# A fourth place for raw U tiles during the selection, paid for with two smaller buffers

## The chip, the cores and the metric

The kernel runs on one core of a Trainium2 chip. What counts is the device time of one execution in microseconds (us); the median of three runs is compared. The engines are named as the profile names them: PE (TensorE matmul), PEld (its weight loads, which overlap), DVE (VectorE), ACT (ScalarE), POOL (GpSimd) and SP (SyncE, which issues most of the transfers).

## The reference, cut to what matters

Two trunk layers of a decoder run over 544 tokens (512 of a prompt, 32 of samples). Each layer is a mixer block followed by PEER, a layer of 16384 single-neuron experts of which every token picks 128. The change lies in PEER alone:

```python
q = (h @ w_q).reshape(B, T, PEER_HEADS, 2, PEER_HALF)
s = jnp.einsum('bthpc,hpkc->bthpk', q, subkeys)
s_top, i_top = lax.top_k(s, PEER_TOPK)            # 16 of 128 keys, for each half
...
best, pos = lax.top_k(cand, PEER_TOPK)            # 16 of the 256 pairs
idx = jnp.take_along_axis(cidx, pos, axis=-1)     # expert = key1 * 128 + key2
gate = jax.nn.softmax(best, axis=-1)
...
a = jnp.einsum('td,thed->the', xb, jnp.take(U, ib, axis=0))
wgt = gb * jax.nn.gelu(a)
return jnp.einsum('the,thed->td', wgt, jnp.take(V, ib, axis=0))
```

## The kernel before, in words

PEER treats its tokens in two ways. The first 384 tokens go through all experts densely: `gelu(U h)` is computed for each of the 128 tiles of U (tile k holds the 128 experts whose second key is k), multiplied by a matrix G of gates that is zero where an expert was not picked, and multiplied by V. The other 160 tokens fetch the rows of U and V that they picked, with indirect transfers from POOL (`gather`, five row buffers `g_r` of 128 x 1024 f32, 4 KB a partition each).

In each layer the order is as follows. `scores` computes the keys' scores and first top-16 lists. `second_stage` picks the 16 pairs of each head; it runs once for the gathered tokens and then three times, for 128 dense tokens each. After each of these three, `make_g` builds the columns of G: for 16 chunks of 8 tokens DVE makes four f16 tiles of 2 KB a partition: `ohp` (first key's one-hots), `ohq` (second key's), `ohh` and `ohl` (`ohq` times the high and the low part of the gate). PE multiplies `ohp` with `ohh` and `ohl` (L1467, L1468). `ohq` is read by DVE alone. The results pass through the tile `stage` to DRAM (`gd`), and through DRAM back into `gt`.

This stretch is called the selection here. To keep PE busy in it, `spend` strews two other kinds of work into the program: U tiles (`a_early`) and steps of the gather. A U tile is one transfer of 512 KB into a raw tile `wr` (L105, from SP), one cast `wh` on ACT (L98), one difference `wl` on DVE (L99), and 24 matmuls on PE (L118). `wr` has three places, `wh` and `wl` two each. The result passes through gelu (L1020) into the tile `kept` or, in groups of four, to DRAM (`ad`, L1027). The first 8 raw tiles of U are loaded beforehand into places of their own (`pre`). After the last `make_g` a loop runs `a_early` until 96 tiles are done (L1116 to L1117); the other 32 are done in the dense stage.

The dense stage takes the 128 tiles of V, one a step: a raw tile `vr` (L1183, three places), its split `vh`, `vl` (two places each), a gated tile of activations split into `gwh`, `gwl`, and 18 matmuls (L1199). Activations that went to DRAM come back as `gr` (L1168) with their gates `gt` (L1165). In the gather, `use` forms the dot products of the rows of U with h (L1268): the products are written to the tile `g_junk`, which nobody reads; the sum over the row goes to one column of `g_w`.

The kernel is written for a framework that places tiles in memory pool by pool, adds the waits, and writes each engine's instructions in an order that a planner fixes when the kernel is built; the planner may take an instruction ahead of earlier ones. On the chip every engine, and SP's queue of transfers, works strictly in that order. A tile that lies where an earlier, closed pool lay waits for the last use of what lay there.

The pools of the selection lie one on the other from `vi` (`val`, `idx`) over `sp` (the second stage's tiles) to `mg` (`make_g`'s tiles: four small ones, `stage` twice 16 KB, then the one-hots). When they are closed, the dense stage's pools take the place from the bottom of `vi` on: `fn` (two accumulators of 4 KB), `dv` (`vr` 3 x 4 KB, `vh` 2 x 4 KB, `vl` 2 x 4 KB), `dn` (`gwh`, `gwl`, `gt`, `gr`).

Of the kernel before, what the change touches and what calls it, by code (L numbers as in the profile page):

```python
# [9 lines left out]
F32 = mybir.dt.float32  # L10
F32R = mybir.dt.float32r
F16 = mybir.dt.float16
U32 = mybir.dt.uint32
AF = mybir.ActivationFunctionType
OP = mybir.AluOpType
AX = mybir.AxisListType

P = 128
L = 2
D = 1024  # L20
# [15 lines left out]
NKEY = 128  # L36
# [43 lines left out]
class Body:  # L80
# [917 lines left out]

    def a_fetch(self):
        k = self.a_next  # L1000
        self.a_w = self.weights(self.a["u"][self.a_l, k], wr=self.pre.pop(k, None)) if k < NKEY else None

    def a_tile(self, psum, ahead):

# [41 lines left out]
    def peer(self, l):  # L1046
        nc, a = self.nc, self.a
        gd = self.dp.tile([ND // ST, P, P, ST], F32, name=f"gd{l}")
        self.ad = self.dp.tile([P, NKEY // GA, GA, ND], F32, name=f"ad{l}")
        self.a_l, self.a_next, self.a_w = l, 0, None  # L1050
        self.pre = {}
        self.rows_due, self.rows_left = None, ROWPRE
        self.t_dve = self.t_pe = self.t_row = 0.0
        with ExitStack() as es:
# [7 lines left out]
            ve = ExitStack()  # L1062
# [3 lines left out]
            sp = self.pool("sp", ve)  # L1066
            ge = ExitStack()

            with ExitStack() as es2:
                hb = self.pool("hb", es2)  # L1070

                bh = hb.tile([P, NK, NQ], F32R, name="bh")
                bl = hb.tile([P, NK, NQ], F32R, name="bl")

                with ExitStack() as es3:
                    ns = self.pool("ns2", es3)
                    g = self.gains(ns, "g_ffn", l)

                    def sink(i, xt):
                        np_ = TILE[i]  # L1080
                        h = self.rownorm(ns, [xt], np_, g)
                        to = [(bh, bl, (i - 2) * P)] if i > 1 else []
                        to += [(self.ah, self.al, i * P)] if i < 3 else []

                        def put(k, pt):
                            for hi, lo, c in to:
                                self.split(hi[:, k:k + 4, c:c + np_], lo[:, k:k + 4, c:c + np_], pt)

                        self.to_feat(h, np_, 0, put)
                        if i == 3:  # L1090
                            nc.sync.dma_start(self.h2d[l][0], h)
                        elif i == 4:
                            for q in range(4):
                                nc.sync.dma_start(self.h2d[l][1, q * TS:(q + 1) * TS], h)

                    self.out_proj(l, ns, sink)
                self.hxs.close()
                sc = self.pool("sc", es2)
                pp = self.pool("pre", es2, side="right")
                self.pre = {k: pp.tile([P, D], F32, name=f"pre{k}") for k in range(PRE)}  # L1100
                self.scores(l, sc, val, idx, bh, bl)
                self.t_pe = 1e9
                self.second_stage(sp, val[:, 24:], idx[:, 24:], last)
                while self.pre:
                    self.a_early(len(self.pre) > 1)
            with ExitStack() as es2:
                mg = self.pool("mg", es2)
                gp = self.pool("gp", ge, side="right")
                self.rows_due = self.gather(l, gp, acc, last)
                self.t_dve = self.t_pe = self.t_row = 0.0  # L1110
                for i in range(ND // P):
                    F = [sp.tile([P, PH, TOPK], F32, name=f"sel{s}") for s in range(3)]
                    self.second_stage(sp, val[:, i * 8:i * 8 + 8], idx[:, i * 8:i * 8 + 8], F)
                    self.make_g(l, mg, gd, i, F)
            while self.a_next % GA or self.a_next < APRE:
                self.a_early(self.a_next % GA != GA - 1)  # L1116
            ve.close()  # L1117
            fn = self.pool("fn", es)
            acc += [fn.tile([P, D], F32, name=f"g_acc{i}") for i in range(2)]
# [117 lines left out]
    def gather(self, l, gp, acc, last):  # L1237

        nc, a = self.nc, self.a
        h2t = []  # L1240
        for t in range(2):
            h2t.append(gp.tile([P, D], F32, name=f"h2t{t}"))
            nc.sync.dma_start(h2t[t], self.h2d[l][t])
        u, v = [], []
        for t, (b0, b1) in enumerate(((0, PH), (PH, PH + 2))):
            ns = (b1 - b0) * TOPK
            src = [x[:, b0:b1].rearrange("p h k -> p (h k)") for x in last]
            ef = gp.tile([P, ns], F32, name=f"g_ef{t}")
            nc.vector.tensor_scalar(ef, src[0], float(NKEY), float(l * NKEY * NKEY), op0=OP.mult, op1=OP.add)
            e = gp.tile([P, ns], mybir.dt.int32, name=f"g_e{t}")  # L1250
            nc.vector.tensor_add(e, ef, src[1])
            w = gp.tile([P, ns], F32, name=f"g_w{t}")
            for s in range(ns):
                u.append((0, t, s, e, w, src[2]))
                v.append((1, t, s, e, w, src[2]))
        jobs = u + v
        rows = []
        late = None

        def use(job, r):  # L1260
            nonlocal late
            which, t, s, e, w, g = job
            if late is not None and s % TOPK == 2:
                nc.vector.tensor_mul(*late)
                late = None
            if which == 0:
                jk = gp.tile([P, D], F16, name="g_junk", bufs=1)
                ins = nc.vector.scalar_tensor_tensor(jk, r, 1.0, h2t[t], op0=OP.mult, op1=OP.mult,  # L1268
                                                     accum_out=w[:, s:s + 1])
                self.tc.keep_in_program_order(ins)  # L1270
                if s % TOPK == TOPK - 1:
                    ws = w[:, s + 1 - TOPK:s + 1]
                    nc.scalar.activation(ws, ws, AF.Gelu_apprx_tanh)
                    late = (ws, ws, g[:, s + 1 - TOPK:s + 1])
            else:
                nc.vector.scalar_tensor_tensor(acc[t], r, w[:, s:s + 1], acc[t], op0=OP.mult, op1=OP.add)  # L1276

        def run():
            for n in range(len(jobs) + GR - 1):
                if n < len(jobs):  # L1280
                    which, t, s, e, w, g = jobs[n]
                    r = gp.tile([P, D], F32, name="g_r", bufs=GR)
                    nc.gpsimd.indirect_dma_start(out=r, out_offset=None,  # L1283
                                                 in_=a["v" if which else "u_rows"].rearrange("l e d -> (l e) d"),
                                                 in_offset=bass.IndirectOffsetOnAxis(ap=e[:, s:s + 1], axis=0))
                    rows.append(r)
                if n >= GR - 1:
                    use(jobs[n - GR + 1], rows.pop(0))
                yield

        return run()
# [141 lines left out]
    def make_g(self, l, sp, gd, i, F):  # L1433
# [13 lines left out]
        for c in range(0, P, OHT):  # L1447
            if c % ST == 0:
                stage = sp.tile([P, P, ST], F32, name="stage", bufs=2)

            sh = [P, OHT // 2, P, 2]

            def row(t):
                return t[:, c:c + OHT].rearrange("p (b t) -> p b t", t=2)[:, :, None, :].to_broadcast(sh)

            keys = self.io[:, None, :, :].to_broadcast(sh)
            p_, q_, qh, ql = (sp.tile(sh, F16, name=n, bufs=2) for n in ("ohp", "ohq", "ohh", "ohl"))
            nc.vector.tensor_tensor(p_, keys, row(i1), op=OP.is_equal)
            nc.vector.tensor_tensor(q_, keys, row(i2), op=OP.is_equal)
            nc.vector.tensor_tensor(qh, q_, row(gh), op=OP.mult)  # L1460
            nc.vector.tensor_tensor(ql, q_, row(gl), op=OP.mult)
            self.spend(dve=2.9)
            for b in range(0, OHT, 4):
                ps = self.bank(2).rearrange("p (t j) -> p t j", t=4)
                for t in range(4):
                    w, half = (b + t) // 2, t % 2
                    nc.tensor.matmul(ps[:, t], p_[:, w, :, half], qh[:, w, :, half], start=True, stop=False)  # L1467
                    nc.tensor.matmul(ps[:, t], p_[:, w, :, half], ql[:, w, :, half], start=False, stop=True)  # L1468
                o = (c + b) % ST
                nc.scalar.activation(stage[:, :, o:o + 4].rearrange("p j t -> p t j"), ps,  # L1470
                                     AF.Copy, scale=1.0 / GSCALE)
            self.t_pe += 1.0
            if (c + OHT) % ST == 0:
                t = i * P + c + OHT - ST
                k = self.kept[:, :, t:t + ST]
                nc.vector.tensor_mul(k, k, stage[:, :KJ])
                nc.scalar.dma_start(gd[t // ST, :, KJ:], stage[:, KJ:])
# [128 lines left out]
```

## Time and profile before

| | before |
|---|---|
| median of 3 runs | 3926.21 us (3915.0 to 3933.97) |
| profiled execution: time / span | 3939.12 us / 3937.3 us |
| PE busy | 3796.4 us, 96% |
| PEld busy | 3423.2 us, 87% |
| DVE busy | 2885.8 us, 73% |
| ACT busy | 1579.2 us, 40% |
| POOL busy | 1084.3 us, 28% |
| DMA | 936.55 MB, mean 238 GB/s |
| mean granted TensorE clock | 0.987 |

A busy share is an average over stages that have different limits, so the stretch in which a change works has to be looked at by itself. The selection of the first layer lies at about 880 to 1320 us of the span, that of the second at about 2810 to 3250 us; the dense stages follow each.

### The profile page before, as it was taken

Reading aid. Unit: us, or ns where it says so; the run is one execution under the profiler, and the core shown is the slowest. Engines: PE = TensorE matmul, PEld = TensorE weight load, DVE = VectorE, ACT = ScalarE, POOL = GpSimd, SP = SyncE. Lnnn points to the kernel's source line nnn. Section 1 sums busy time; section 2 is a strip of 40 time slices with the busy share of each in tenths; the row PEclk is TensorE's granted clock in tenths of the full one; section 3 lists DMA queues with packets and bytes.
Section 4 is the critical chain, followed back from the end, with each engine's and each line's share of the span. In section 5 each row is a group of like instructions: output and inputs, shape, how many; then the busy total and the mean of one; then the engine's idle time right before and its main releaser. Section 6 shows DMA issues by size and latency. Waiting matters only on the chain.

```text
span 3937.3 us, 66183 instructions
## 1 busy us (share of the span) xinstructions
PE 3796.4 (96%) x25676; PEld 3423.2 (87%) x25676; DVE 2885.8 (73%) x5799; ACT 1579.2 (40%) x2373; POOL 1084.3 (28%) x880
## 2 busy tenths in 40 slices
PE   8999999999999899999999999999999989999998
PEld 7999997999989788888789998879989888888886
DVE  5554436799998787888955444467999878788888
ACT  4532324344555333333344323343456543333333
POOL 0110100005353444444501110000164334444343
PEclk9999999999999999999999999999999999999999
DMA  7243215327889999999933322262478999999997
GB/s 261 87 145 109 66 55 192 137 70 276 307 302 354 348 359 331 337 354 350 383 127 126 128 87 63 76 239 70 152 284 290 336 364 349 343 338 344 346 349 280
DMA packets 334028, 936.55 MB, mean 238 GB/s; under 512 B 28784, under 2 KB 126448, under 8 KB 330384
## 3 DMA queue, kind: packets, MB, share of 16 engines
q1 hardware_dynamic: 232912, 527.52, 38.5%
q0 software_dynamic: 92160, 335.59, 23.3%
q10 hardware_dynamic: 8640, 69.21, 4.5%
q8 instruction: 201, 3.29, 0.3%
q14 instruction: 115, 0.94, 0.1%
HBM read 835.50 MB, written 96.70 MB: 237 GB/s over the span
## 4 chain that ended last, share of the span: by engine, by line
PE 83%; DVE 6%; DMA 5%; issue 3%; ACT 2%; SPq 1%; POOL 1%; DVEq 0%; POOLq 0%; ACTq 0%
PE mm L118 36%; PE mm L1199 17%; PE sm L1199 8%; PE sm L118 7%; DMA g_r<-u_rows,g_e 3%; PE mm L344 2%; PE sm L586 2%; DVE wl L99 1%; SPq L1168 1%; PE sm L1467 1%; PE sm L1468 1%; PE sm L529 1%; PE sm L1340 1%; POOL g_r L1283 1%; PE sm L344 0%
## 5 line engine op out<-in xcount | busy, mean ns | idle before, releaser
L1283 POOL DMA_INDIRECT g_r<-u_rows,g_e x320 | 532.1, 1663 | 1322.9 <-DVE g_junk L1268 596.6
L98 ACT CAST wh<-wr 128x1024 fp32r<-128x1024 f32 (+1 forms) x464 | 466.2, 1005 | 945.5 <-PE mm L118 694.7
L99 DVE TENSOR_TENSOR wl<-wr,wh 128x1024 fp32r<-128x1024 f32 (+1 forms) x464 | 541.4, 1167 | 383.0 <-ACT wh L98 360.1
L118 PE MATMUL mm<-ah,wh 128*128 128x384 f32 (+1 forms) x1792 | 599.8, 335 | 29.3 <-ACT wh L98 22.8
L118 PE MATMUL mm<-ah,wl 128*128 128x384 f32 (+1 forms) x1792 | 603.1, 337 | 18.8 <-DVE wl L99 18.5
L118 PE MATMUL mm<-al,wh 128*128 128x384 f32 (+1 forms) x1792 | 594.3, 332 | 0.4 <-DVE al L99 0.4
L1283 POOL DMA_INDIRECT g_r<-v,g_e x320 | 440.6, 1377 | 525.8 <-DVE g_acc L1276 479.2
L1268 DVE SCALAR_TENSOR_TENSOR g_junk<-g_r,h2t 128x1024 f16<-128x1024 f32 x320 | 391.1, 1222 | 31.0 <-DMA g_r<-u_rows,g_e 29.7
L1276 DVE SCALAR_TENSOR_TENSOR g_acc<-g_r,g_w,g_acc 128x1024 f32<-128x1024 f32 x320 | 409.5, 1280 | 1.8 <-DMA g_r<-v,g_e 0.2
L118 PEld LDWEIGHTS mm<-ah,wh 128*128 128x128 f32 x1792 | 344.1, 192 | 37.1 <-ACT wh L98 24.9
L118 PEld LDWEIGHTS mm<-ah,wl 128*128 128x128 f32 x1792 | 343.0, 191 | 30.2 <-DVE wl L99 29.5
L118 PEld LDWEIGHTS mm<-al,wh 128*128 128x128 f32 x1792 | 343.7, 192 | 0.9 <-DVE al L99 0.9
L99 DVE TENSOR_TENSOR vl<-vr,vh 128x1024 fp32r<-128x1024 f32 x256 | 312.4, 1221 | 38.3 <-ACT vh L98 37.2
L118 PE MATMUL mm<-hh,wl 128*128 128x272 f32 x1536 | 332.4, 294 | 0.0
L118 PE MATMUL mm<-hl,wh 128*128 128x272 f32 x1536 | 330.9, 293 | 0.0
L118 PE MATMUL mm<-hh,wh 128*128 128x272 f32 x1536 | 328.5, 294 | 0.2 <-ACT hh L98 0.2
L1199 PE MATMUL mm<-vl,gwh 128*128 128x512 f32 x1024 | 317.4, 391 | 2.1 <-DVE vl L99 2.1
L1199 PE MATMUL mm<-vh,gwl 128*128 128x512 f32 x1024 | 316.3, 390 | 0.0
L1199 PE MATMUL mm<-vh,gwh 128*128 128x512 f32 x1024 | 281.0, 393 | 18.7 <-ACT vh L98 18.7
L98 ACT CAST vh<-vr 128x1024 fp32r<-128x1024 f32 x256 | 268.2, 1051 | 0.3 <-DMA vr<-v 0.3
L98 ACT CAST gwh<-gr 128x384 fp32r<-128x384 f32 x144 | 74.0, 514 | 447.9 <-PE sm L1199 447.9
L118 PEld LDWEIGHTS mm<-hl,wh 128*128 128x128 f32 x1536 | 242.8, 188 | 8.8 <-issue 6.7
(476 smaller groups left out, 7503.9 us busy)
## 6 DMA issues: line engine op xcount, KB each, us to landing
vr<-v SPq DMA_DIRECT2D x256, 512.0 KB, 6.8
wr<-u SPq DMA_DIRECT2D x240, 512.0 KB, 5.8
wr<-w_in SPq DMA_DIRECT2D x96, 512.0 KB, 3.5
gd<-stage ACTq DMA_DIRECT2D x24, 1664.0 KB, 8.9
gt<-gd SPq DMA_DIRECT2D x52, 768.0 KB, 7.8
ad<-ga ACTq DMA_DIRECT2D x36, 768.0 KB, 7.1
gr<-ad SPq DMA_DIRECT2D x36, 768.0 KB, 8.1
wr<-w_o SPq DMA_DIRECT2D x32, 512.0 KB, 3.5
```

The source lines that it names most:

```text
L98: self.nc.scalar.copy(hi, src)
L99: self.nc.vector.tensor_sub(lo, src, hi.bitcast(F32))
L118: nc.tensor.matmul(o, w[:, k * P:(k + 1) * P], x[part][:, k], start=(q == 0), stop=(q == 3 * nk - 1))
L344: nc.tensor.matmul(ps[i][s][:np_], m[:, k, c], w[:, s * 512:(s + 1) * 512], start=(k == 0 and q == 0), stop=(k == NK - 1 and q == 2))
L529: nc.tensor.matmul(ps[i], x[:, k, i * P:(i + 1) * P], w[:, kk * BW:(kk + 1) * BW], start=(k == 0 and q == 0), stop=(k == NK - 1 and q == 2))
L586: self.pairs_of(lambda b, lo, hi: nc.tensor.matmul(p[lo:hi, b], w[lo:hi, b], x(b, lo, hi), start=True, stop=True))
L1168: nc.sync.dma_start(ga4, self.ad[:, q])
L1199: ins = nc.tensor.matmul(po[i][s], w[:, i * P:(i + 1) * P], v[:, s * 512:(s + 1) * 512], start=(step == 1 and m == 0), stop=(step == NKEY ...
L1268: ins = nc.vector.scalar_tensor_tensor(jk, r, 1.0, h2t[t], op0=OP.mult, op1=OP.mult, accum_out=w[:, s:s + 1])
L1276: nc.vector.scalar_tensor_tensor(acc[t], r, w[:, s:s + 1], acc[t], op0=OP.mult, op1=OP.add)
L1283: nc.gpsimd.indirect_dma_start(out=r, out_offset=None, in_=a["v" if which else "u_rows"].rearrange("l e d -> (l e) d"), in_offset=bass.Ind ...
L1340: nc.tensor.matmul(ps[:, j, half], q[:, half, (i + j) * P:(i + j + 1) * P], sub[:, h * 2 + half], start=True, stop=True)
```

## The change

Three edits. A new pool `raw` with one tile of 128 x 1024 f32 (4 KB a partition) is opened between `sp` and `mg`. While it is open, every fourth tile of U (k = 11, 15, ... 95) is loaded into it instead of into one of the three places of `wr`. Its space comes from two others: `ohq` gets one buffer in place of two (2 KB), and `g_junk` (2 KB) goes away, the products of L1268 being written over the row `g_r` that they were formed from, in f32. `raw` is closed together with `vi` and `sp`, before the dense stage.

```diff
@@ a_fetch
         k = self.a_next
-        self.a_w = self.weights(self.a["u"][self.a_l, k], wr=self.pre.pop(k, None)) if k < NKEY else None
+        wr = self.pre.pop(k, None)
+        if wr is None and k < NKEY and k % 4 == 3 and self.raw is not None:
+            wr = self.raw.tile([P, D], F32, name="raw")
+            self.nc.sync.dma_start(wr, self.a["u"][self.a_l, k])
+        self.a_w = self.weights(self.a["u"][self.a_l, k], wr=wr) if k < NKEY else None
@@ peer
-        self.pre = {}
+        self.pre, self.raw = {}, None
...
                 while self.pre:
                     self.a_early(len(self.pre) > 1)
+
+            self.raw = self.pool("raw", ve)
             with ExitStack() as es2:
                 mg = self.pool("mg", es2)
...
             while self.a_next % GA or self.a_next < APRE:
                 self.a_early(self.a_next % GA != GA - 1)
+            self.raw = None
             ve.close()
@@ gather, use
-                jk = gp.tile([P, D], F16, name="g_junk", bufs=1)
-                ins = nc.vector.scalar_tensor_tensor(jk, r, 1.0, h2t[t], op0=OP.mult, op1=OP.mult,
+                ins = nc.vector.scalar_tensor_tensor(r, r, 1.0, h2t[t], op0=OP.mult, op1=OP.mult,
                                                      accum_out=w[:, s:s + 1])
@@ make_g
-            p_, q_, qh, ql = (sp.tile(sh, F16, name=n, bufs=2) for n in ("ohp", "ohq", "ohh", "ohl"))
+            p_, qh, ql = (sp.tile(sh, F16, name=n, bufs=2) for n in ("ohp", "ohh", "ohl"))
+            q_ = sp.tile(sh, F16, name="ohq")
```

## Rows read from the trace of the kernel before

**Rows 1.** The page's first line of engines: busy us (share) x instructions.
```profile
PE 3796.4 (96%) x25676; PEld 3423.2 (87%) x25676; DVE 2885.8 (73%) x5799; ACT 1579.2 (40%) x2373; POOL 1084.3 (28%) x880
```

**Rows 2.** Stretches of the first selection: length, busy by engine, clock, DMA share, GB/s.
```profile
960.00:980.00 20.00, 19.95 (x149) 18.70 (x148) 20.00 (x32) 14.11 (x18) 16.99 (x2) 1.00 0.63 227
...
1120.00:1140.00 20.00, 13.50 (x84) 12.72 (x84) 14.14 (x24) 6.30 (x9) 10.57 (x8) 0.83 0.89 327
...
1220.00:1240.00 20.00, 20.00 (x159) 19.37 (x158) 19.85 (x30) 13.15 (x17) 4.61 (x5) 1.00 0.91 335
```

**Rows 3.** Who waited for whom, 860 to 1325 us: total us, times, longest.
```profile
ACT wh L98 <- PE mm L118: 163.1, 72, 9.3
...
DVE g_junk L1268 <- DMA g_r<-u_rows,g_e: 16.0, 5, 5.9
...
ACT wh L98 <- DMA wr<-u: 12.7, 3, 8.4
...
PE sm L1467 <- DVE ohh L1460: 6.5, 1, 6.5
```

**Rows 4.** The passage to the dense stage, both layers: columns as in rows 2.
```profile
1265.00:1280.00 15.00, 12.89 (x61) 11.90 (x60) 7.10 (x8) 5.14 (x7) 4.72 (x3) 0.89 1.04 387
1280.00:1291.00 11.00, 2.08 (x8) 1.06 (x6) 3.37 (x6) 2.18 (x3) 0.00 (x0) 0.77 1.06 381
1291.00:1323.00 32.00, 30.49 (x157) 29.68 (x158) 24.23 (x36) 7.71 (x12) 14.80 (x12) 0.92 1.02 361
...
3212.00:3223.00 11.00, 2.74 (x9) 1.67 (x8) 3.69 (x6) 2.52 (x3) 0.00 (x0) 0.77 1.06 382
```

**Rows 5.** SP's queue in that passage, first layer: start, us, instruction, count.
```profile
1255.31 0.33 SPq L105 DMA_DIRECT2D wr<-u  x1
...
1257.53 15.95 SPq L1168 DMA_DIRECT2D gr<-ad  x1
...
1274.01 5.91 SPq L1168 DMA_DIRECT2D gr<-ad  x1
1280.02 0.97 SPq L105 DMA_DIRECT2D wr<-u  x2
1281.08 0.48 SPq L1183 DMA_DIRECT2D vr<-v  x1
```

**Rows 6.** ACT there: start, us, instruction, idle before and what ended it.
```profile
1288.52 1.04 ACT L98 CAST wh<-wr 128x1024 fp32r<-128x1024 f32 x1 [8.43 <-DMA wr<-u]
```

**Rows 7.** The chain that ended last: one U tile on PE.
```profile
1239.92 4.22 PE mm L118 x24
```

**Rows 8.** The dense stage's matmuls (L1199) alone in the passage: length, PE, PEld, clock, DMA.
```profile
1265.00:1280.00 15.00, 2.15 (x9) 1.79 (x10) 0.89 1.04 387
1280.00:1291.00 11.00, 0.95 (x5) 0.44 (x3) 0.77 1.06 381
```

**Rows 9.** DVE by line and shape: busy us, mean ns, idle before.
```profile
L99 DVE TENSOR_TENSOR wl<-wr,wh 128x1024 fp32r<-128x1024 f32 x416 | 508.6, 1223 | 371.7 <-ACT wh L98 348.9 <-ACT d_wt L662 16.8 <-PE sm L118 3.0
...
L1268 DVE SCALAR_TENSOR_TENSOR g_junk<-g_r,h2t 128x1024 f16<-128x1024 f32 x320 | 391.1, 1222 | 31.0 <-DMA g_r<-u_rows,g_e 29.7
...
L173 DVE SCALAR_TENSOR_TENSOR n_h<-x_o,rs_y,g_row 128x1024 f32<-128x1024 f32 x8 | 10.1, 1282 | 0.0
```

**Rows 10.** DVE in time: two chunks of make_g, first layer.
```profile
948.97 1.29 DVE L1459 TENSOR_TENSOR ohq<-io,i2T 128x1024 f16<-128x1024 f16 x2
...
955.02 1.29 DVE L1461 TENSOR_TENSOR ohl<-ohq,glT 128x1024 f16<-128x1024 f16 x2
```

**Rows 11.** DVE in time, after the second second_stage of the first layer.
```profile
994.25 1.23 DVE L1268 SCALAR_TENSOR_TENSOR g_junk<-g_r,h2t 128x1024 f16<-128x1024 f32 x1 [4.61 <-DMA g_r<-u_rows,g_e]
```

**Rows 12.** POOL in time, in two windows of the first selection.
```profile
964.85 25.61 POOL L1283 DMA_INDIRECT g_r<-u_rows,g_e  x1 [2.78 <-DVE gsum L1386]
...
1094.99 28.13 POOL L1283 DMA_INDIRECT g_r<-u_rows,g_e  x1 [3.93 <-DVE g_junk L1268]
```

**Rows 13.** A stretch of the first dense stage: columns as in rows 2.
```profile
1400.00:1500.00 100.00, 100.00 (x476) 86.52 (x475) 79.61 (x120) 33.40 (x47) 43.26 (x33) 1.00 0.97 350
```

## The prediction

> **What bounds the kernel now.** I read the page first: PE is busy for 96% of the span and no other engine for more than 87% [rows 1], so a change pays only where it fills a gap of PE. Next I cut the first selection into stretches of 20 us. PE and DVE are both full or nearly so in most of them, as at 960 and 1220 us, and 1120 to 1140 us is one of the few with a hole [rows 2]. The list of waits then says what raw tiles of U have to do with that: ACT's cast waits 72 times, 163.1 us, for PE to give back a place of `wh`, and only three times, 12.7 us, for the raw tile itself [rows 3]. So in the steady part the raw tile lies ready; three places are enough there. By SP's queue, the three late tiles all belong to the passage into the dense stage, after the last `make_g`. There PE is idle for 15.00 - 12.89 = 2.11, 11.00 - 2.08 = 8.92 and 32.00 - 30.49 = 1.51 us, 12.5 us in the first layer, and the granted clock falls (0.89, 0.77, 0.92: parts of the stretches run at 1.2 in place of 2.4 GHz); the second layer repeats it, with 8.26 us in the stretch in the middle [rows 4]. The queue shows why: one U tile leaves at 1255.31, then come the first loads of the dense stage, two `gr` among them that hold the queue for 15.95 and 5.91 us, and the next two U tiles leave at 1280.02 [rows 5]. DMA engines are full in this time (share 1.04 to 1.06 [rows 4]). ACT sits 8.43 us for that tile [rows 6], and PE behind it.
>
> **The fourth place.** A U tile costs PE 4.22 us [rows 7]. With four places the transfer of tile k waits for the split of tile k-4 in place of k-3, so each U tile stands one place further forward in SP's queue. Nothing is added to what is moved: the tile that leaves at 1255.31 is simply the next one by number. In the steady part this is worth nothing; what hides it is the wait of the cast for PE [rows 3]. At its first use, tile 11, the place waits for the scores' operand that lay there; the three tiles in `wr` before it cover that. Before the hold it gives PE one more tile to do: -4.2 us a layer.
>
> It also takes something away. In units of a partition's bytes, `vi` is 8704 and `sp` 14304, so `raw` lies from 23008 to 27104. The dense stage puts `fn` (8192) and three `vr` (12288) below, so its two `vh` lie from 20480 to 28672, and `raw` is under both. The last tile of the selection, 95, is a `raw` tile (95 = 3 mod 4). So the first two steps of the dense stage can't cast V before tile 95 has been split. Today some of their matmuls fill the hole: 2.15 + 0.95 = 3.1 us of PE in the two stretches [rows 8]. They will come later: +3.1 us. What is queued behind: `vl` on DVE and the next `vr`, which wait for these casts; the planner knows this wait and can put U's casts and loads ahead, so I add nothing for them. In turn those `vr`, as at 1281.08 [rows 5], no longer share the full DMA engines with U's tiles. Below, this is worth nothing; above, no more than the idle time that is left of the middle stretch, 8.9 - 4.2 + 3.1 = 7.8 us. Only two of the transfers then under way go, so I take a sixth, -1.3 us. Together: -4.2 + 3.1 - 1.3 = -2.4 us a layer, -4.8 us in both.
>
> What comes after keeps this gain: in the dense stage PE is busy for 98 to 100 of 100 us [rows 13], so work done earlier ends earlier.
>
> **One buffer for the second key's one-hots.** Writer and readers of `ohq` are all on DVE, which works in order, so no wait between engines is added. What changes is the order. Now `ohq` of two chunks is written in a row before either `ohl` [rows 10]; by DVE's rows 25 of the 48 chunks of a layer have it so. These must move behind the previous `ohl`. DVE's work is the same. Bounds a layer: if PE waited for every moved one, 25 times half of 1.29 us [rows 10], +16 us; if the new order took away PE's one long wait for `ohh`, -6.5 us [rows 3]. The rows stand near to zero: in 48 chunks PE has one long wait of this kind, and it comes when DVE itself stands for a gathered row. I take 0.
>
> **Products written over the rows.** 320 instructions write f32 where they wrote f16, in place. With f16 one takes 1222 ns; a difference of two f32 tiles written in f32-sized words takes 1223; a product with a column of scalars, written as f32, 1282 [rows 9]. So it is between 0 and 60 ns each, 0 to 19 us of DVE in all. L1268 has no column operand, so I take 0. The row buffer is given back by the same instruction as before, so the gather's transfers don't wait longer.
>
> **Sum.** 3939.1 us for the profiled execution, less 4.8, is 3934.3. That execution lies 12.9 us above the median of the three runs, so I expect a median of 3926.2 - 4.8 = 3921.4, say 3921. The three runs lie 0.5% apart, and 0.5% (20 us) is about what a measurement here can tell from no change.
>
> **Rivals.** *Faster: the whole hole closes.* If the one tile bridges the hold, because U's later tiles land sooner with the two V loads out of the way, the 12.5 us go, and with them what the low clock costs while PE works: 0.11 x 12.89 + 0.23 x 2.08 + 0.08 x 30.49 = 4.3 us [rows 4]. That is 16.8 us a layer, 34 in both: about 3892. For it speaks that the hole has one cause and stands in the same place in both layers. Against it: the hold lasts from 1257.5 to 1280 and its transfers take until 1288.5 [rows 5, 6], and one tile is half of the 8.43 us. The Trainium skill has a rule for it ("Perfetto Trace Analysis", section "Optimization Strategy"): the same gap coming back on the engine that should be full can mean that there is no room for the next tile. By that rule the hole would close; the trace agrees in that the place was missing, and differs in that the queue and the DMA engines are full as well. I give this 20%.
>
> *Slower: DVE starves the gather once more.* After the second and third `second_stage` one indirect transfer takes 25.61 and 28.13 us on POOL [rows 12], while DVE is busy without a pause [rows 2]; the first ends only after DVE has run out of gathered rows, stands for 4.61 us [rows 11], and PE with it. At the third, PE loses 6.50 us in 1120 to 1140 us, and the clock falls to 0.83, which costs 0.17 x 13.5 = 2.3 us more [rows 2]: some 9 us. The move of 25 `ohq` a layer makes a new order on DVE. If that packs its work so that one more row is held up for longer than the five buffers last, it costs 9 us a layer, 18 in both, and if it does so twice, 36: 3939 to 3957 with the gain above. The Trainium skill gives a mechanism ("SBUF - State Buffer", section "SBUF: two separate sides"): some DVE instructions hold a port that GpSimd needs to write the descriptors of its own transfers. The trace agrees with that for the two long transfers, but does not show which order brings it on. DVE's total work is the same, which speaks against; 14%.
>
> *No use at all.* The planner may place U's loads where they were, or the 3.1 us and the new wait for tile 95 may eat the 4.2 us: 3926, or 3938 if the f32 products cost 60 ns each where DVE is full, in the 97 of a layer that fall in the selection (5.8 us a layer). 26%, within 0.5%.
>
> The forecast itself has 40%; its own range is 3910 to 3932.
>
> **Numbers.** Of the faster rival about all lies more than 0.5% (below 3907) off, and of the forecast a twentieth: 22%. Of the slower rival some three quarters lie above 3946: 11%, and with a little from the third rival 12%. The rest, 66%, is within 0.5%. The range leaves out half of the faster rival and half of the slower one or a little less: 3896 to 3944.
>
> **What would show it.** Right: in SP's queue one more U tile before the first `gr`; PE's idle time in the passage 1 to 5 us a layer smaller, not gone; no L1199 before the split of tile 95; L1268 at 1.22 us; the waits of ACT for `wr` in the steady part still none. Wrong: the hole gone together with the low clock; a fourth POOL transfer of over 20 us in a selection, or PE waits for `ohh` that come in every chunk; L1268 at 1.28 us.

## The result, and the profile after

| | before | after |
|---|---|---|
| median | 3928.57 us (6 runs) | 4016.06 us (4002.09 to 4021.05, 6 runs) |
| ratio to before, 95% interval | 1 | 1.0227 [1.0208, 1.0246] |
| profiled span | 3937.3 us | 4014.7 us |
| mean granted clock | 0.987 | 0.978 |

The change costs 2.3%, some 88 us or 44 us a layer, where 3921 us were forecast with a range that ended at 3944. The engines do the same instructions (the page's line of engines, after; [rows 1]):

```profile
PE 3841.8 (96%) x25676; PEld 3445.2 (86%) x25676; DVE 2890.7 (72%) x5799; ACT 1582.8 (39%) x2373; POOL 1019.2 (25%) x880
```

DVE works no more than before (2890.7 and 2885.8 us). The instruction that was rewritten is not slower either. By line and shape, after (L1268 has become L1274):

```profile
L1274 DVE SCALAR_TENSOR_TENSOR g_r<-g_r,h2t 128x1024 f32<-128x1024 f32 x320 | 384.7, 1216 | 18.0 <-DMA g_r<-u_rows,g_e 17.9
```

So neither the amount of DVE's work nor its price has changed; its order has. The windows of single lines show it. First the gather's products in the first selection, before and then after: length, DVE busy, instructions (two a step: the product and the read-out of its sum), clock, DMA share, GB/s.

```profile
880.00:1240.00 360.00, 91.62 (x150) 0.97 0.83 300
1240.00:1400.00 160.00, 63.87 (x104) 0.96 0.98 356
```

```profile
880.00:1240.00 360.00, 140.36 (x232) 0.98 0.93 340
1240.00:1400.00 160.00, 12.01 (x20) 0.88 0.62 227
```

Then the last one-hots of `make_g`'s chunks (`ohl`, one instruction a chunk), before and after:

```profile
880.00:1240.00 360.00, 32.38 (x48) 0.97 0.83 300
1240.00:1400.00 160.00, 0.00 (x0) 0.96 0.98 356
```

```profile
880.00:1240.00 360.00, 19.03 (x28) 0.98 0.93 340
1240.00:1400.00 160.00, 13.66 (x20) 0.88 0.62 227
```

Up to 1240 us DVE does 116 steps of the gather where it did 75, 48.7 us more, and 28 chunks where it did 48. Twenty chunks of four instructions take 4 x 13.35 = 53.4 us, so the one took the place of the other. The splits of U's tiles hardly moved (69 and 70). The gather's share of the selection (120 fetched rows, the constant `ROWPRE`) is then used up, the 96 tiles of U are done at 1297 us (1319 before), and the last 16 chunks of `make_g` stand alone until 1349 us (all were done at 1245 before). Stretches after, columns as in [rows 2]:

```profile
1240.00:1298.00 58.00, 57.68 (x389) 54.14 (x387) 24.64 (x29) 29.69 (x37) 0.00 (x0) 1.00 0.48 172
1298.00:1350.00 52.00, 34.60 (x279) 28.89 (x280) 44.79 (x70) 32.03 (x37) 0.00 (x0) 0.64 0.39 157
3265.00:3322.00 57.00, 38.23 (x308) 32.17 (x307) 45.76 (x71) 34.04 (x39) 0.00 (x0) 0.67 0.38 152
```

POOL does nothing in all three: the next row has to wait for DVE to give one back, and DVE's next step of the gather stands behind the chunks. In the first, PE has U's tiles and DVE is more than half idle (busy for 24.64 of 58 us). In the second PE has only chunks, most of which wait for DVE, and most of the time its clock is at the lower of its two levels (mean 0.64, where 1 is 2.4 and 0.5 is 1.2 GHz). The second layer repeats it. Who waited for whom from 1270 to 1365 us, after:

```profile
POOL g_r L1289 <- DVE g_r L1274: 134.5, 1, 134.5
...
PEld L1474 <- DVE ohh L1467: 17.7, 13, 5.4
PE sm L1474 <- DVE ohh L1467: 14.5, 13, 5.1
```

One wait of this kind was there before [rows 3]; now 13 of the last 16 chunks have one. The groups of PE show what it adds up to in both layers, before and then after (busy, mean ns, idle before):

```profile
L1467 PE MATMUL sm<-ohh,ohp 128*128 128x128 f16 x768 | 101.2, 221 | 13.5 <-DVE ohh L1460 13.5
L1468 PE MATMUL sm<-ohl,ohp 128*128 128x128 f16 x768 | 94.2, 220 | 0.0
```

```profile
L1474 PE MATMUL sm<-ohh,ohp 128*128 128x128 f16 x768 | 125.9, 243 | 29.3 <-DVE ohh L1467 29.2
L1475 PE MATMUL sm<-ohl,ohp 128*128 128x128 f16 x768 | 116.6, 241 | 7.1 <-DVE ohl L1468 7.1
```

`make_g`'s matmuls are 47.1 us longer (at the low level) and have 22.9 us more idle time before them: 70 of the 77.4 us by which the spans of the two profiled executions differ. What this work displaces is the dense stage. Its matmuls alone (L1199, then L1206) in two stretches, before and after; columns PE, PEld, clock, DMA:

```profile
1240.00:1320.00 80.00, 6.00 (x24) 4.47 (x24) 0.91 1.01 367
1320.00:1365.00 45.00, 33.14 (x138) 25.88 (x139) 1.00 0.92 334
```

```profile
1240.00:1320.00 80.00, 0.00 (x0) 0.00 (x0) 0.91 0.50 183
1320.00:1365.00 45.00, 0.82 (x4) 0.86 (x5) 0.75 0.49 184
```

At 1365 us PE is 39.1 - 0.8 = 38 us of the dense stage behind, and that stage ends 41 us later (2039 and 1998 us).

### The profile page after: what moved, and what is told of

The parts are those of the page before. It is cut to its first block, busy times and chain, and to the rows that moved or that the text cites. A ratio compares the mean times of both kernels' runs of the same rounds, so it can differ in the third digit from the quotient of the medians.

```text
span 4014.7 us, 65879 instructions
## 1 busy us (share of the span) xinstructions
PE 3841.8 (96%) x25676; PEld 3445.2 (86%) x25676; DVE 2890.7 (72%) x5799; ACT 1582.8 (39%) x2373; POOL 1019.2 (25%) x880
## 4 chain that ended last, share of the span: by engine, by line
PE 81%; DVE 10%; issue 3%; DMA 3%; ACT 2%; POOL 1%; SPq 0%; DVEq 0%; POOLq 0%; ACTq 0%
PE mm L118 34%; PE mm L1206 17%; PE sm L1206 8%; PE sm L118 7%; PE mm L344 2%; DVE wl L99 2%; PE sm L586 2%; DVE g_r L1274 2%; POOL g_r L1289 1%; DMA g_r<-u_rows,g_e 1%; PE sm L1475 1%; DVE ohh L1467 1%; DVE ohp L1465 1%; PE sm L1474 1%; DVE ohq L1466 1%
## 5 line engine op out<-in xcount | busy, mean ns | idle before, releaser
L1289 POOL DMA_INDIRECT g_r<-u_rows,g_e x320 | 448.4, 1401 | 1408.1 <-DVE g_r L1274 692.6
L98 ACT CAST wh<-wr 128x1024 fp32r<-128x1024 f32 (+1 forms) x420 | 420.3, 1001 | 913.9 <-PE mm L118 684.2
L99 DVE TENSOR_TENSOR wl<-wr,wh 128x1024 fp32r<-128x1024 f32 (+1 forms) x420 | 486.5, 1158 | 400.2 <-ACT wh L98 379.5
L1289 POOL DMA_INDIRECT g_r<-v,g_e x320 | 459.3, 1435 | 507.3 <-DVE g_acc L1282 466.5
L1274 DVE SCALAR_TENSOR_TENSOR g_r<-g_r,h2t 128x1024 f32<-128x1024 f32 x320 | 384.7, 1216 | 18.0 <-DMA g_r<-u_rows,g_e 17.9
L99 DVE TENSOR_TENSOR vl<-vr,vh 128x1024 fp32r<-128x1024 f32 x256 | 311.8, 1221 | 59.8 <-ACT vh L98 58.6
L1206 PE MATMUL mm<-vl,gwh 128*128 128x512 f32 x1024 | 318.0, 392 | 7.5 <-DVE vl L99 7.5
L1206 PE MATMUL mm<-vh,gwl 128*128 128x512 f32 x1024 | 316.8, 391 | 0.0
L1206 PE MATMUL mm<-vh,gwh 128*128 128x512 f32 x1024 | 281.4, 395 | 20.9 <-ACT vh L98 20.8
L118 PEld LDWEIGHTS mm<-hh,wh 128*128 128x128 f32 x1536 | 245.6, 191 | 6.5 <-issue 3.4
```

Of the source, the lines that this page charges most:

```text
L98: self.nc.scalar.copy(hi, src)
L99: self.nc.vector.tensor_sub(lo, src, hi.bitcast(F32))
L118: nc.tensor.matmul(o, w[:, k * P:(k + 1) * P], x[part][:, k], start=(q == 0), stop=(q == 3 * nk - 1))
L1206: ins = nc.tensor.matmul(po[i][s], w[:, i * P:(i + 1) * P], v[:, s * 512:(s + 1) * 512], start=(step == 1 and m == 0), stop=(step == NKEY ...
L1274: ins = nc.vector.scalar_tensor_tensor(r, r, 1.0, h2t[t], op0=OP.mult, op1=OP.mult, accum_out=w[:, s:s + 1])
L1289: nc.gpsimd.indirect_dma_start(out=r, out_offset=None, in_=a["v" if which else "u_rows"].rearrange("l e d -> (l e) d"), in_offset=bass.Ind ...
```

## Experiments

Sixteen kernels ran. "Steps" are the gather's steps that DVE has done by 1240 us in the first layer (half the count of the windows above). The intervals are 95%; 0.1% is 4 us.

| run | what differs from the kernel before | median us | ratio to before | steps |
|---|---|---|---|---|
| after | rows, ohq, raw | 4016.06 | 1.0227 [1.0208, 1.0246] | 116 |
| e1 | rows | 3994.47 | 1.0181 [1.0138, 1.0225] | 115 |
| e2 | ohq | 3930.01 | 1.0007 [0.9989, 1.0024] | 97 |
| e3 | rows, ohq | 3995.31 | 1.0168 [1.0130, 1.0206] | 116 |
| e4 | as after, ROWSTEP 4.5 | 3950.97 | 1.0058 [1.0035, 1.0081] | 79 |
| e5 | KEEP 5 | 3951.48 | 1.0060 [1.0039, 1.0082] | 77 |
| e6 | KEEP 5, raw | 3931.84 | 1.0026 [1.0010, 1.0041] | 77 |
| e7 | KEEP 5, two g_junk | 3977.28 | 1.0130 [1.0096, 1.0164] | 114 |
| e8 | KEEP 5, one g_junk in f32 | 3951.11 | 1.0062 [1.0038, 1.0086] | 74 |
| e9 | raw, ohq, one g_junk in 8 bits | 3941.10 | 1.0029 [1.0012, 1.0046] | 95 |
| e10 | as after, APRE 104 | 4023.21 | 1.0236 [1.0198, 1.0275] | 116 |
| e11 | KEEP 5, three g_junk | 3989.95 | 1.0146 [1.0108, 1.0184] | 111 |
| e12 | KEEP 5, rows | 4003.84 | 1.0183 [1.0144, 1.0221] | 112 |
| e13 | as e9, APRE 100 | 3937.99 | 1.0035 [1.0017, 1.0053] | 95 |
| e14 | GR 4, raw | 3982.85 | 1.0157 [1.0114, 1.0200] | 80 |
| e15 | GR 4 | 3983.86 | 1.0154 [1.0114, 1.0195] | 77 |
| e16 | KEEP 5, raw, ohq | 3949.41 | 1.0071 [1.0053, 1.0089] | 94 |

The chips differ a little (before had medians of 3919 to 3929 us), so ratios are compared.

**Which edit (e1, e2, e3).** e1 is the kernel before with the one instruction changed:

```diff
-                jk = gp.tile([P, D], F16, name="g_junk", bufs=1)
-                ins = nc.vector.scalar_tensor_tensor(jk, r, 1.0, h2t[t], ...
+                ins = nc.vector.scalar_tensor_tensor(r, r, 1.0, h2t[t], ...
```

> Only the products of U's rows are written over the rows; g_junk is gone; ohq keeps two buffers and there is no raw place. Theory 'pace': the one buffer of g_junk held the planner to about one step of the gather for each chunk of make_g. Without it, steps come in pairs, make_g is pushed back, and the U tiles run out before it. Then most of the 88 us should be here: between make_g's 48 chunks 70 to 80 steps of the gather (56 before, 79 after), make_g ended 40 us or more later than before, and 3965 to 4010 us. Rival 'raw place': 3915 to 3940, as before. Rival 'ohq': 3915 to 3940, as before.

e2 has the one buffer of `ohq` alone:

```diff
-            p_, q_, qh, ql = (sp.tile(sh, F16, name=n, bufs=2) for n in ("ohp", "ohq", "ohh", "ohl"))
+            p_, qh, ql = (sp.tile(sh, F16, name=n, bufs=2) for n in ("ohp", "ohh", "ohl"))
+            q_ = sp.tile(sh, F16, name="ohq")
```

> Only ohq has one buffer; g_junk stays and there is no raw place. Theory 'pace': the gather keeps its one step a chunk, and make_g ends late by little; 3925 to 3950 us. Rival 'ohq' (the single buffer alone slows make_g until PE starves): 3980 to 4020. Rival 'raw place': 3915 to 3940.

e3 has both diffs, without the pool `raw`:

> Both buffers given up, but no raw place is made of them: the changed kernel without its fourth place. Theory 'pace': as slow as the changed kernel, 3995 to 4025 us, with 75 or more steps of the gather between make_g's chunks and chunks at the end with no U tile beside them. Rival 'raw place' (the fourth place and the waits it brings cost the time): back to 3915 to 3945.

The products over the rows cost 1.8% by themselves, the single `ohq` nothing, both together what the first costs, and `raw` on top of both another 0.6%. In e1 DVE is the limit: from 1000 to 1240 us it has no pause at all, and PE waits in front of U's tiles. The stretch and two groups of PE in e1:

```profile
1000.00:1240.00 240.00, 221.00 (x1538) 205.99 (x1536) 240.00 (x371) 125.38 (x161) 110.04 (x75) 0.99 0.93 350
```

```profile
L118 PE MATMUL mm<-ah,wl 128*128 128x384 f32 (+1 forms) x1792 | 603.4, 338 | 38.1 <-DVE wl L99 37.2
L118 PE MATMUL mm<-ah,wh 128*128 128x384 f32 (+1 forms) x1792 | 601.3, 336 | 30.1 <-ACT ga L1020 20.8 <-ACT kept L1016 8.3
```

Before, the wait for `wl` came to 18.5 us:

```profile
L118 PE MATMUL mm<-ah,wl 128*128 128x384 f32 (+1 forms) x1792 | 603.1, 337 | 18.8 <-DVE wl L99 18.5
```

In e1 more of the price is paid along the way, in the changed kernel at the end; what the two have in common is the 40 steps done early. e2 did not go as I expected in its order: 97 steps by 1240 us and `make_g` finished at 1304 us, 59 us later than before. But there U's tiles went ahead too (the 96 are done at 1285 us, 1319 before), so PE had work, and the time is that of before. Neither a late `make_g` alone nor 22 early steps cost anything there.

**What in that edit (e5, e7, e8, e11, e12).** Two things go with the scratch tile: the store becomes f32 and lands in the row, and a tile of one buffer disappears. The planner puts the gather and U's tiles ahead of `make_g` where it finds buffers free. While there is only one `g_junk`, one step of the gather is never put right behind another: before, none of the 75 products up to 1240 us follows straight on the one ahead of it, and the same holds in every version with one `g_junk`. In the changed kernel 20 of 116 do, in e1 31. One such pair (DVE in time, after):

```profile
1107.28 1.22 DVE L1274 SCALAR_TENSOR_TENSOR g_r<-g_r,h2t 128x1024 f32<-128x1024 f32 x1
1108.43 0.08 DVE L1274 DVE_READ_ACCUMULATOR g_r<-g_r,h2t 128x1 f32 x1
1108.43 1.22 DVE L1274 SCALAR_TENSOR_TENSOR g_r<-g_r,h2t 128x1024 f32<-128x1024 f32 x1
```

Whether this is what costs the time is the next question. To have space for the opposite trial, KEEP was lowered to 5 (five kept groups of activations), and the base run again:

```diff
-KEEP = 6
+KEEP = 5
```

> The kernel before with five tiles of activations kept in place of six (KEEP = 5), which frees 4 KB a partition and changes nothing else. It is the base that the next three are compared with. All theories: within 0.5% of the kernel before, 3910 to 3945 us; one gather step beside each chunk of make_g as before, make_g of the first layer ends at 1235 to 1260 us.

The base itself came out 0.6% slower, just outside what was expected (3951 us, where all theories ended at 3945). On it, an f32 scratch tile with its one buffer:

```diff
-                jk = gp.tile([P, D], F16, name="g_junk", bufs=1)
+                jk = gp.tile([P, D], F32, name="g_junk", bufs=1)
```

> KEEP = 5 and the one buffer of g_junk in f32: the store is as wide as in the changed kernel, the single buffer stays. Theory pace: within 0.5% of the KEEP = 5 kernel, the instruction at 1215 to 1225 ns, one gather step a chunk. Rival (the f32 store costs): 3960 us or more.

```profile
L1268 DVE SCALAR_TENSOR_TENSOR g_junk<-g_r,h2t 128x1024 f32<-128x1024 f32 x320 | 390.9, 1221 | 21.3 <-DMA g_r<-u_rows,g_e 20.0
```

1221 ns and the base's time (1.0062 against 1.0060): no cost of the wide store is seen. Now more buffers, in f16 and with the rows left alone, and last the products over the rows (the diff of e1) on the same base:

```diff
-                jk = gp.tile([P, D], F16, name="g_junk", bufs=1)
+                jk = gp.tile([P, D], F16, name="g_junk", bufs=2)
```

(`bufs=3` in e11.)

> KEEP = 5 and two buffers of g_junk, products written in f16 as before; nothing is written over the rows. Theory pace (the one buffer of g_junk kept the planner from putting a gather step right behind another, and its removal let the gather run at double pace): about 79 of the gather's steps between the first and the last chunk in pairs, make_g of the first layer ends at 1325 to 1350 us, PE 92 to 96% busy or less in 880 to 1200 us, time 3970 to 4010 us like the version with the products over the rows alone. Rival (the f32 write over the row costs by itself, by its port, its bytes or by the row's later release): within 0.5% of the KEEP = 5 kernel.

> KEEP = 5 and three buffers of g_junk, f16, nothing written over the rows. Theory pace: the more buffers, the further the gather runs ahead; with three the order comes near to that of the products over the rows, and the time lies above that of two buffers (3977 us) and near to that of the next run. Rival (writing over the row has a cost of its own on the chip): the next run lies 20 us or more above this one.

> KEEP = 5 and the products over the rows, nothing else. Theory pace: like three buffers of g_junk within 15 us, 3980 to 4020 us. Rival (the write over the row costs by itself): 20 us or more above three buffers.

A second buffer costs 26 us although no instruction has been added, and the steps by 1240 us go from 77 to 114. It isn't the space either: two f16 buffers take the same 4 KB as the one f32 buffer of e8. With one, two, three buffers and none needed at all the medians are 3951, 3977, 3990 and 4004 us. So the time follows the number of buffers, but the count of early steps does not follow it all the way: it is 114, 111 and 112 in the last three, and why they still differ is open. Between e11 and e12 the medians differ by 14 us, and all four runs of e12 lie above all four of e11 (4001 to 4006 and 3986 to 3998 us). A cost of its own for the write over the row could be that much; whether it is that or the order was not tried.

**Giving the brake back (e9, e4).** e9 is the changed kernel with a scratch tile of one buffer again, small enough to fit:

```diff
-            ef = gp.tile([P, ns], F32, name=f"g_ef{t}")
+            ef = src[0]
...
+                jk = gp.tile([P, D], mybir.dt.float8e4, name="g_junk", bufs=1)
```

> The changed kernel with its scratch tile given back: the raw place and the one buffer of ohq stay, the products go to a g_junk of one buffer again, in 8-bit floats (1 KB a partition; nobody reads it); the float expert number g_ef (640 bytes) is formed in its source, so that six kept tiles fit. Theory pace (all of the loss is the missing one-buffer tile): the gather goes singly again, about 97 steps between the first and the last chunk as with ohq alone, and the place of raw tiles pays as it did beside KEEP = 5: 3905 to 3930 us. Rival (the raw place and the single ohq together cost some 20 us): 3940 to 3960 us. Rival (the change's other parts cost as well): 3980 us or more.

75 of the 88 us come back. What is left, 0.3%, lies at the low edge of the first rival and outside the theory's 3905 to 3930 us: the expected gain of `raw` isn't there. In e4 the spacing of the steps in the program was raised instead:

```diff
-ROWSTEP = 2.5
+ROWSTEP = 4.5
```

> The changed kernel with the constant that spaces the gather's steps in the program raised from 2.5 to 4.5 (ROWSTEP), nothing else. Theory 'pace': the program's spacing takes the place of the lost buffer; under 60 steps between make_g's chunks, make_g and the 96th U tile end within 15 us of each other, and nearly all of the loss comes back: 3900 to 3950 us. Rival 'raw place' and rival 'ohq': the time stays at 3990 or above, since neither depends on the gather.

The gather is back at 79 steps by 1240 us, and three quarters of the loss are gone, without any scratch tile. (Between the first and the last chunk there were still 78 steps, not fewer than 60 as expected, and `make_g` ended 28 us after the 96th tile of U, not within 15. The steps come later, and that goes with the time.)

**The stretch without U's tiles (e10, e13).** If the hole at 1298 to 1350 us came from too few tiles of U, eight more should fill it:

```diff
-APRE = 96
+APRE = 104
```

> The changed kernel with 104 in place of 96 tiles of U before the dense stage (APRE). Theory that part of the loss is that U's tiles are used up before make_g ends (1298 to 1350 us: PE 34.6 of 52 us busy at a mean clock of 0.64, 29 us a layer): eight more tiles of 4.2 us fill the most of it, 3960 to 3995 us. Rival (DVE's work is what limits the whole selection, so more splits on DVE only push make_g further back): 4005 us or more.

No gain. Two stretches of e10, all engines and then `ohl` alone:

```profile
1240.00:1320.00 80.00, 80.00 (x527) 75.60 (x526) 38.52 (x47) 38.61 (x51) 0.00 (x0) 1.00 0.56 204
1320.00:1360.00 40.00, 30.54 (x253) 26.53 (x251) 33.48 (x50) 27.21 (x31) 0.00 (x0) 0.77 0.39 155
```

```profile
1240.00:1320.00 80.00, 4.55 (x7) 1.00 0.56 204
1320.00:1360.00 40.00, 7.07 (x11) 0.77 0.39 155
```

The extra tiles were put ahead of the chunks, so the hole came later. My rival had the time right and the reason wrong: DVE was busy for 38.5 of 80 us there. It is the order that leaves the chunks to the end. e13, four more tiles (`APRE = 100`) in e9, agrees (1.0035 against 1.0029):

> The version with the raw place, one ohq and the one-buffer scratch tile, with 100 in place of 96 tiles of U before the dense stage. Theory that the raw place costs beside the single ohq because U's tiles end before make_g (1275 against 1318 us; PE 22.8 of 40 us at clock 0.55 in 1280 to 1320 us): four tiles, 17 us of PE, fill part of that stretch, 10 to 30 us below that version's 3941 us. Rival (the hole only moves to a later place, as it did with 104 tiles in the changed kernel): within 10 us of 3941 us or above.

**The fourth place by itself (e6, e16, e14, e15).** e6 is e5 with the pool `raw` and the change in `a_fetch`, nothing else:

```diff
+            wr = self.raw.tile([P, D], F32, name="raw")
+            self.nc.sync.dma_start(wr, self.a["u"][self.a_l, k])
```

> KEEP = 5 and the fourth place of raw U tiles alone: g_junk and two buffers of ohq stay. The step of the prediction: one more U tile before the first gr, the passage 1 to 5 us a layer shorter, no L1199 matmul before tile 95 is split; time 0 to 10 us below the KEEP = 5 kernel, about -5. Theory that the raw place itself costs (after stands 20 us above the version with both other edits and no raw place): 10 to 25 us above the KEEP = 5 kernel. Theory that the 20 us come only where the gather has run ahead: no loss here.

Here one part of the forecast's mechanism can be seen, and another not. SP's queue in e5 and in e6, where `vr` are loads of V and L1004 is the fourth place:

```profile
1239.68 4.22 SPq L1183 DMA_DIRECT2D vr<-v  x3
1244.00 0.47 SPq L105 DMA_DIRECT2D wr<-u  x1
...
1245.10 17.37 SPq L1168 DMA_DIRECT2D gr<-ad  x1
...
1263.16 4.03 SPq L1168 DMA_DIRECT2D gr<-ad  x1
1267.29 0.85 SPq L105 DMA_DIRECT2D wr<-u  x2
```

```profile
1246.19 5.21 SPq L1175 DMA_DIRECT2D gr<-ad  x1
...
1251.97 10.32 SPq L105 DMA_DIRECT2D wr<-u  x1
1262.34 0.43 SPq L1175 DMA_DIRECT2D gr<-ad  x1
1262.87 0.38 SPq L1004 DMA_DIRECT2D raw<-u  x1
1263.35 0.90 SPq L105 DMA_DIRECT2D wr<-u  x2
...
1289.62 1.72 SPq L1190 DMA_DIRECT2D vr<-v  x3
```

One more tile of U ahead of the first `gr` was forecast. It isn't there: 82 have left by then in e5 and in e6 alike, in both layers. What has changed is the order around it. Three loads of V that stood ahead of the first `gr` now leave behind tile 95, and the first `gr` holds the queue for 5.21 in place of 17.37 us. A tile of U now stands second and is held itself for 10.32 us, but four of them are on their way by 1264.3 us, where none left from 1244.5 to 1267.3 us. That the missing loads of V are what shortens the hold is likely, but no run tried it alone. PE in the passage, e5 and e6:

```profile
1265.00:1320.00 55.00, 39.08 (x196) 36.27 (x195) 31.87 (x49) 13.31 (x20) 20.19 (x14) 0.88 0.99 349
```

```profile
1265.00:1320.00 55.00, 49.83 (x259) 47.89 (x260) 36.48 (x51) 19.30 (x26) 16.09 (x14) 0.91 1.01 374
```

That is 10.75 us more of PE in this stretch of the first layer. The gain is 0.34% by the ratios (13 us), 19.6 us by the medians. With the single `ohq` added (the diff of e2), it is gone:

> KEEP = 5, the raw place and one buffer of ohq; g_junk as before, in f16. Theory that the raw place loses its gain beside the single ohq: 10 us or more above KEEP = 5 with the raw place and two ohq (3932 us). Rival (the 14 us left in the version with the scratch tile in 8-bit floats come from that tile or from g_ef, not from ohq): within 8 us of 3932 us or below.

So the place's gain goes without any 8-bit tile, which makes the pair of `raw` and the single `ohq` the likely source of what e9 still loses; e9 with its tile in f16 was not run. The group of PE in e2 (no `raw`) and in e9, and the stretch at the end of `make_g` in both:

```profile
L1468 PE MATMUL sm<-ohh,ohp 128*128 128x128 f16 x768 | 105.9, 222 | 14.7 <-DVE ohh L1461 14.6
```

```profile
L1475 PE MATMUL sm<-ohh,ohp 128*128 128x128 f16 x768 | 115.9, 233 | 39.6 <-DVE ohh L1468 39.6
```

```profile
1280.00:1320.00 40.00, 32.20 (x210) 30.81 (x209) 26.54 (x40) 18.55 (x25) 9.67 (x8) 0.87 0.90 332
```

```profile
1280.00:1320.00 40.00, 22.81 (x159) 19.69 (x160) 33.24 (x57) 16.07 (x18) 14.16 (x12) 0.55 0.76 267
```

With the fourth place U's tiles end at 1274 us in e9 (1285 in e2), while `make_g` runs to 1318 us (1304): the faster supply empties the stock that the late chunks need beside them. The changed kernel shows the same against e3: U's tiles end at 1297 and 1313 us, `make_g` at 1349 and 1346. A pair was to try `raw` in the order of the kernel before, with KEEP 6, its place paid for with a row buffer; e15 is the kernel before with

```diff
-GR = 5
+GR = 4
```

and e14 adds `raw` as in e6:

> The kernel before with four row buffers, the base of the run before. All theories: a slower gather, 3925 to 3960 us; the gather's transfers of over 20 us on POOL cost more than before, since four rows last less long than five.

> The kernel before with the raw place alone, paid for with one of the five row buffers (GR = 4); six kept tiles, two buffers of ohq and one of g_junk stay. Theory that the raw place pays about 20 us wherever the gather and make_g keep their order: 15 to 25 us below the same kernel without the raw place (next run). Rival (it pays only beside KEEP = 5): within 8 us of the next run.

The pair comes out within 1 us, the rival's mark, but it decides nothing: both lie above the 3925 to 3960 us expected of the base, and with four rows the gather of V's rows became the bound. In e15 the dense stage's matmuls end at 3924.5 us, but PE waits for the gather, and the span is 3972.6 us (waits of e15, 3850 us to the end):

```profile
ACT gr L153 <- PE sm L1232: 37.6, 1, 37.6
...
PEld sm L1232 <- DVE g_acc L1276: 29.0, 1, 29.0
```

In e14 the first layer's dense stage ends 14 us earlier than in e15 (1960.0 and 1973.9 us), and the rows eat it. No version that ran beats the kernel before.

## Why the prediction was wrong

- **What failed is the step "Products written over the rows".** It priced the instruction (0 to 60 ns, taken 0) and asked whether the row is given back later. Both answers were right: 1216 ns, and no longer wait for rows. That the order would stay was taken without a word, and that was wrong: e1 has this edit alone and costs 1.8%. `g_junk` was looked at as a place for bytes that nobody reads. It also kept one gather step from being placed right behind another (none of 75 before, 31 of 115 in e1), and with it gone some 40 steps a layer moved from the passage and the start of the dense stage, where DVE has room [rows 13], into the selection, where it has none [rows 2]. Their 48.7 us of DVE were within the prediction's reach: 40 x 1.22 us [rows 9].
- **One buffer for `ohq`: the number was right (0; measured 0.07%, interval -0.11 to 0.24%), its reason was not.** I argued that DVE's work is the same and that 25 `ohq` must move. In fact the whole selection was put in another order (steps between the first and the last chunk 57 before, 97 in e2). So that the number came out right is luck: this order costs nothing only where U's tiles go ahead with the gather and still reach to the last chunks, and beside `raw` it costs (e6 to e16: 0.45%, 18 us).
- **The fourth place: a gain as forecast, but from another term of the sum.** Alone (e5 to e6) it gives 13 to 20 us where the sum had 4.8. The term of one more tile before the hold, 4.2 us, isn't there (82 tiles in both). The mis-sized term is the one for V's loads, taken as a sixth of the middle stretch, 1.3 us: with them gone from ahead of the first `gr`, the hold is 12 us shorter and four tiles pass. The dense stage's first matmuls do come behind tile 95 (1256.7 us in e5, 1310.7 in e6), as foreseen. But the forecast took the passage as a place whose surroundings stay. In the changed kernel U's tiles are done 60 us before the first `gr` (1297 and 1357.9 us), and the place has nothing left to gain there; with rows and `ohq` it costs 0.6% more (e3 to after).
- **The rivals.** *Slower: DVE starves the gather* foresaw a new order on DVE and a loss, but not this one: no transfer of POOL took more than 14.95 us in the selection's 880 to 1200 us, against 25.61 and 28.13 [rows 12]. *The whole hole closes* did not come. The Trainium skill ("Perfetto Trace Analysis", section "Optimization Strategy") says that the same gap coming back can mean that the next tile has no room. In e6 the trace agrees: room for that tile shortened the gap. That is no rule for other tiles: in e7 a second buffer for a scratch tile lost 26 us. *No use at all* had the f32 store as a cost; e8 shows none.
- **What would show it.** Three signs of "right" came true in the slow kernel (more tiles of U ahead of the first `gr`, 94 against 83; no L1206 before tile 95; L1274 at 1.22 us). They tested the pieces and not the order between them. The one that spoke, PE waiting for `ohh` in chunk after chunk, stood under "wrong".

What stays open: whether the write over the row has a small cost of its own (e11 to e12, 14 us); why two and three buffers of `g_junk` and none needed differ at nearly the same count of early steps; and how `raw` would pay with six kept groups, two `ohq` and five rows, which was not run.

## What to carry to other kernels

Where an order is made by a planner that runs ahead as far as buffers let it, every count of buffers can also be a brake, and here that of a scratch tile which nobody reads set the pace: before taking it away, ask what could not be placed twice in a row because of it. Price such an edit by what the freed stream would displace (steps times their duration, on the engine that is full in that stretch), not by the instruction. And when a buffer has to go, put an explicit pace in its place (a small tile of one buffer, or a wider spacing): e9 and e4 got 75 and 65 of 88 us back that way.

## What the runs showed of the hardware

- DVE without a pause is not enough to hold up POOL's indirect transfers. In e1 DVE is busy for 240.00 of 240 us, and the longest transfer in it is this one (POOL in time, e1):

```profile
1153.95 4.74 POOL L1282 DMA_INDIRECT g_r<-u_rows,g_e  x1 [0.30 <-DVE ohq L1458]
```

  Before, one took 28.13 us in the same stretch [rows 12], with DVE busy for 229.20 of 240. The Trainium skill ("SBUF - State Buffer", section "SBUF: two separate sides") names some DVE instructions, not a busy DVE, as what locks POOL out. No run here shows which ones they would be.
- The width and the place of this instruction's store make no difference on DVE: 1216 ns in f32 over its own operand (after), 1221 ns in f32 beside it (e8), 1222 ns in f16 [rows 9], 1217 ns in 8 bits (e9).
- A stretch of short matmuls that wait for DVE pays twice. In the changed kernel, from 1298 to 1350 us, PE is idle for a third of the time, and the granted clock, 1.00 in the 58 us before with PE busy for 57.68 of them, is 0.64 on average; a matmul of `make_g` that takes 0.22 us elsewhere takes 0.31 us there.
